# An MLA encoder layer in split fp32: latent keys and gate by seven products of quarters, rotary queries behind the gates

## The chip, the cores and the metric

The kernel runs on one core of a Trainium2 chip. The metric is the device time of one execution, in microseconds (us); a measurement is the median of its runs. Engines are named as in the profile: PE is TensorE (matrix products), PEld its weight loads, DVE VectorE, ACT ScalarE, POOL GpSimd, SP SyncE, which issues nearly all DMAs.

## The reference

One layer of multi-head latent attention over 1024 tokens of width 1024, with 8 heads, all in fp32:

```python
proj = rms_norm(x, g) @ w_in                  # columns: 384 + 256 + 64 + 1024
c_q, c_kv, k_pe, gate = proj[..., :384], proj[..., 384:640], proj[..., 640:704], proj[..., 704:]
q  = (rms_norm(c_q, q_norm) @ w_uq).reshape(B, L, 8, 192)     # 128 plain + 64 rotary
kv = (rms_norm(c_kv, kv_norm) @ w_ukv).reshape(B, L, 8, 256)  # 128 keys + 128 values
q_pe, k_pe = apply_rope(q_pe), apply_rope(k_pe)               # k_pe is shared by all heads
p = softmax((q_nope @ k_nope.T + q_pe @ k_pe.T) * scale)      # per head, not causal
h = x + ((p @ v) * silu(gate)) @ w_out
out = rms_norm(h, final_norm)
```

## The kernel before

**Number format.** fp32 is carried as two fp32r parts, high and low. `split(raw, hi, lo)` makes the high part by a cast on GpSimd and the low part by `raw - hi` on VectorE; `mm3` forms a product as three matmuls, high x high, high x low, low x high (lines 59, 60, 61). Everything before attention is held transposed: features on the 128 partitions, the 1024 tokens along the free axis, in two halves of 512.

**First stage (4.7 to 38 us).** While x arrives in eight blocks of 128 features, each block is scaled by the layer's gain and split into `xh` and `xl` (128 x 8 x 1024 each), and the three tiles of latent queries are accumulated in six PSUM banks. They are copied out raw into `craw_a`. The row factor of the norm, `rx`, is applied to results later, since it is one number for each token.

**Second stage (38 to 171 us), the one that changes.** Ten tiles of 128 weight columns are streamed from DRAM, two of latent keys and eight of the gate. `stream(m)` loads a tile in two parts (`gwr`), splits it (`gwh`, `gwl`) and does 8 blocks x 2 halves x 3 = 48 matmuls into one PSUM tile of 128 x 1024. ScalarE copies latent keys out to `craw`; `stream_gate` multiplies a gate by `rx_sb` (VectorE, reading PSUM) and applies Silu (ScalarE). Between the tiles stand:

- `rstd_x`: the squares of x by ScalarE, the factor `rx` by small VectorE operations, and `spread`, which turns it into a row on all partitions by writing it to DRAM and reading it back;
- `latent_sums`, `latent_norm`, `latent_scale`: the norms of latent queries and keys, with sums of squares by GpSimd additions and a matmul with ones (`total`), again with hops through DRAM;
- the rotary key (`pe`, 32 matmuls, high weight and low weight side by side), its rotation, `kk_h` and `kk_l`;
- the rotary queries: `rope_half(g, half, w)` is called four times, after gates 1 to 4. Each does 18 matmuls into two PSUM tiles `ab`, four multiplications by cosine and sine (VectorE, reading PSUM), two additions (GpSimd), two copies (ScalarE), two subtractions (VectorE), and writes the results to DRAM by four DMAs, from where attention reads them (`qpe`);
- the splits of latent queries (`cq_h`, `cq_l`) and latent keys (`kv_h`, `kv_l`).

**Attention (171 us on)** starts with the first head's keys, `k<-kv_h,wk_h`, then queries, values, scores, softmax, an exchange by DMA and the product with the values. The output projection, the residual and the final norm end the kernel.

**What sets the order.** The program is written with a tile framework that simulates a timeline and sets each engine's instructions into one fixed sequence from dependencies, priorities (the order of the code) and its own estimates. Tiles come from pools; a tile of a pool that is used up waits until the last reader of the old one is done. Pools here are given room in the order of opening and closing, so a pool that takes the room of another waits for the other's readers too.

Of the kernel before, what the change touches and what calls it, by code (L numbers as in the profile page):

```python
# [29 lines left out]
def kernel(  # L30
# [32 lines left out]
    def split(raw, hi, lo):  # L63
        nc.gpsimd.tensor_scalar(hi, raw, 1.0, 1.0, op0=ALU.mult, op1=ALU.mult)
        nc.vector.tensor_sub(lo, raw, f32(hi))
# [131 lines left out]
    wts = cctx.enter_context(tc.tile_pool(name="wts", bufs=1))
    kvp = cctx.enter_context(tc.tile_pool(name="kvp", bufs=1))
    kv_h = kvp.tile([P, 2, L], F32R, name="kv_h")
    kv_l = kvp.tile([P, 2, L], F32R, name="kv_l")  # L200
    rx_sb = xs.tile([P, L], F32, name="rx_sb")
    small = xs.tile([P, 16, KD], F32, name="small")
    ssx, mx, rx, v_s, s_s, r_s = (small[:, i] for i in range(6))
# [6 lines left out]
        nc.sync.dma_start(row_d[name], compact)  # L210
        nc.sync.dma_start(row, row_of(name).partition_broadcast(P))
# [12 lines left out]

    def latent_sums(ms, name):
        cs, sq = gate[:, 4], gate[:, 5]
        for i, m in enumerate(ms):
            if i == 0:
                nc.scalar.activation(cs, craw[m], AF.Square)
            else:  # L230
                nc.scalar.activation(sq, craw[m], AF.Square)
                nc.gpsimd.tensor_add(cs, cs, sq)
        line = gate[0:1, 6]
        for half in range(2):
            nc.scalar.copy(line[:, halves(half)], total(cs, half, name)[0:1])
        nc.sync.dma_start(row_of(name), line)
# [12 lines left out]
            c = craw[m]  # L249
            nc.vector.scalar_tensor_tensor(c, c, g_sb[:, KD + m:KD + m + 1], row, op0=ALU.mult, op1=ALU.mult)  # L250
# [23 lines left out]
    rstd_x()
    ps = stream(3)
    nc.scalar.copy(craw[3], ps)
    latent_sums((0, 1, 2), "sq")
    ps = stream(4)
    nc.scalar.copy(craw[4], ps)
    latent_norm("sq", QR, "rq", gate[:, 7])  # L280
    latent_sums((3, 4), "sk")

    wr = gp.tile([P, KD, DR], F32, name="wpe_r", tag="gwr", bufs=2)
# [5 lines left out]
    for k in range(KD):  # L291
        w = w_pe[k // 4][:, k % 4].rearrange("p a b -> p (a b)")
        for half in range(2):
            hs = halves(half)
            mm(ps[:, hs], lhsT=w, rhs=xh[:, k, hs], start=k == 0, stop=False)
# [13 lines left out]
    for d in (slice(0, DR), slice(DR, P)):  # L309
        nc.scalar.copy(kk_h[d], kp[0:DR])  # L310
        nc.vector.tensor_sub(kk_l[d], kp[0:DR], f32(kk_h[0:DR]))

    latent_scale((0, 1, 2), gate[:, 7])
    latent_norm("sk", KR, "rk", gate[:, 7])
    cqp = cctx.enter_context(tc.tile_pool(name="cqp", bufs=1))
    cq_h = [cqp.tile([P, L], F32R, name=f"cq_h{m}") for m in range(3)]
    cq_l = [cqp.tile([P, L], F32R, name=f"cq_l{m}") for m in range(3)]
    for m in range(3):
        nc.scalar.copy(cq_h[m], craw[m])
        nc.vector.tensor_sub(cq_l[m], craw[m], f32(cq_h[m]))  # L320
# [23 lines left out]
    def rope_half(g, half, w):  # L344

        hs = halves(half)
        ab = []
        for i in range(2):
            ab.append(acc("ab"))
            for k in range(3):  # L350
                mm3(ab[i], w[i][0][:, k], w[i][1][:, k], cq_h[k][:, hs], cq_l[k][:, hs], k == 0, k == 2)
        cos, sin = rope_sb[:, 0, hs], rope_sb[:, 1, hs]
        for i, (f0, f1, op) in enumerate(((cos, sin, ALU.subtract), (sin, cos, ALU.add))):
            t, hl = rooms[((g * 2 + half) * 2 + i) % len(rooms)]
            t0, t1 = t[:, 0:HT], t[:, HT:L]
            hi, lo = hl[:, 0:HT], hl[:, HT:L]
            nc.vector.tensor_mul(t0, ab[0], f0)
# [3 lines left out]
            nc.vector.tensor_sub(lo.bitcast(F32R), t0, hi)  # L361
            for c, src in ((i, hi), (2 + i, lo)):
                nc.sync.dma_start(qpe_d[g * 4:(g + 1) * 4, c, :, hs], src)

    w_rope = [[load_q(wqp[j], rw) for j in range(2)], None]
    for i in range(1, H):
        stream_gate(i)
        if i == 2:
            w_rope[1] = [load_q(wqp[2 + j]) for j in range(2)]
        if i == 5:  # L370
            latent_scale((3, 4), gate[:, 7])
        if i == 6:
            for m in range(2):
                nc.gpsimd.tensor_scalar(kv_h[:, m], craw[3 + m], 1.0, 1.0, op0=ALU.mult, op1=ALU.mult)
                nc.vector.tensor_sub(kv_l[:, m], craw[3 + m], f32(kv_h[:, m]))
# [430 lines left out]
```

## Time and profile before

| | |
|---|---|
| time, median of three runs | 586.93 us (586.86 to 587.76) |
| profiled execution | 587.4 us, of which the span of instructions is 585.7 |
| TensorE busy | 571.8 us, 98% of the span, 2604 matmuls |
| VectorE busy | 425.4 us, 73% |
| ScalarE busy | 275.5 us, 47% |
| GpSimd busy | 233.8 us, 40% |
| granted TensorE clock, mean over the span | 0.993 |
| HBM | 36.19 MB read, 8.41 MB written |

The page of the profile gives the busy time of each engine and its number of instructions, then the span in 40 equal slices, where a digit is the busy share of a slice in tenths, and last the chain of work that ended last. A row of a single instruction in the trace is: start in us, duration in us, engine, line of the kernel, operation, what it writes, what it reads, shape; in brackets the time for which the engine had stood idle and what ended it. A row of a stretch is: the stretch, its length, then busy time and number of instructions for PE, PEld, DVE, ACT, POOL, the granted clock, the share of the DMA engines, GB/s.

### The profile page before, as it was taken

How to read it: one execution, taken by the hardware profiler on the slowest of the kernel's cores; microseconds unless marked ns; L12 is line 12 of the kernel's file. 1: busy time of each engine (PE TensorE's matmuls, PEld its weight loads, DVE VectorE, ACT ScalarE, POOL GpSimd, SP SyncE). 2: the span in 40 equal slices, each digit the busy share in tenths (PEclk: the TensorE clock that was granted, in tenths of full speed). 3: DMA queues.
4: the chain of work that ended last, by engine and by line, in shares of the span. 5: the costliest groups of instructions: out<-in, count | busy, mean ns of one | idle time of the engine just before them, and what ended most of it. 6: DMA issues, size and time to landing. Idle time of an engine off the chain costs nothing.

```text
span 585.7 us, 7657 instructions
## 1 busy us (share of the span) xinstructions
PE 571.8 (98%) x2604; PEld 472.8 (81%) x2604; DVE 425.4 (73%) x573; ACT 275.5 (47%) x438; POOL 233.8 (40%) x201
## 2 busy tenths in 40 slices
PE   9999999999999999999999999999999979999995
PEld 5888888888888878888888888888888858788885
DVE  4923589475236799988888988898888894984663
ACT  4348463021014455553655455645365662644652
POOL 1623512343102345643553535533434874683000
PEclk9999999999999999999999999999999979999999
DMA  8766221324211448674457464763476458521332
GB/s 263 275 206 245 95 74 38 124 93 141 109 38 46 94 117 193 154 171 109 107 132 179 105 153 109 168 148 94 100 162 147 132 135 213 198 77 54 138 132 107
DMA packets 35962, 78.66 MB, mean 134 GB/s; under 512 B 7314, under 2 KB 11154, under 8 KB 35860
## 3 DMA queue, kind: packets, MB, share of 16 engines
q1 hardware_dynamic: 34628, 76.21, 48.3%
q10 hardware_dynamic: 1296, 1.97, 0.9%
q8 instruction: 20, 0.33, 0.2%
q14 instruction: 18, 0.15, 0.1%
HBM read 36.19 MB, written 8.41 MB: 76 GB/s over the span
## 4 chain that ended last, share of the span: by engine, by line
PE 90%; SPq 3%; DVE 2%; ACT 1%; DMA 1%; issue 1%; POOL 0%; DVEq 0%; ACTq 0%; POOLq 0%
PE g L59 6%; PE g L61 6%; PE g L60 6%; PE o L59 5%; PE o L60 5%; PE o L61 5%; PE pv L60 5%; PE pv L59 5%; PE pv L61 5%; PE s L59 4%; PE s L60 4%; PE s L459 4%; PE s L61 4%; PE s L458 4%; SPq L481 3%; PE q L59 2%
## 5 line engine op out<-in xcount | busy, mean ns | idle before, releaser
L472 POOL TENSOR_SCALAR probs<-probs,rc 128x1024 f32<-128x1024 f32 x64 | 84.3, 1319 | 113.0 <-DVE rc L471 108.9
L466 ACT ACTIVATE probs<-s,nmx 128x1024 f32<-128x1024 f32 x64 | 71.6, 1118 | 113.3 <-DVE nmx L464 110.4
L473 DVE STREAM_TRANSPOSE probs<-probs 128x1024 f32<-128x1024 f32 x64 | 79.2, 1238 | 15.8 <-POOL probs L472 14.2
L464 DVE TENSOR_REDUCE nmx<-s 128x1 f32<-128x1024 f32 x64 | 76.0, 1207 | 3.8 <-PE s L459 3.7
L488 ACT CAST pt_h<-d 128x1024 fp32r<-128x1024 f32 x64 | 65.3, 1052 | 8.0 <-PE pv L61 4.9
L59 PE MATMUL g<-xh,gwh 128*128 128x512 f32 x160 | 62.2, 389 | 0.0
L60 PE MATMUL g<-xl,gwh 128*128 128x512 f32 x160 | 62.2, 389 | 0.0
L61 PE MATMUL g<-xh,gwl 128*128 128x512 f32 x160 | 62.2, 389 | 0.0
L493 POOL TENSOR_TENSOR pt_l<-d,pt_h 128x512 fp32r<-128x512 f32 x32 | 49.1, 1534 | 26.0 <-ACT pt_h L488 25.3
L60 PE MATMUL pv<-pt_l,v_h 128*128 128x512 f32 x128 | 50.3, 393 | 2.4 <-POOL pt_l L493 2.0
L59 PE MATMUL s<-k_h,q_h 128*128 128x512 f32 x128 | 50.2, 392 | 1.2 <-ACT probs L466 1.2
L490 DVE TENSOR_TENSOR pt_l<-d,pt_h 128x1024 fp32r<-128x1024 f32 x32 | 48.8, 1524 | 3.5 <-ACT pt_h L488 3.3
L59 PE MATMUL pv<-pt_h,v_h 128*128 128x512 f32 x128 | 50.1, 392 | 0.0
L60 PE MATMUL s<-k_l,q_h 128*128 128x512 f32 x128 | 49.9, 390 | 0.0
L61 PE MATMUL pv<-pt_h,v_l 128*128 128x512 f32 x128 | 49.9, 389 | 0.0
L61 PE MATMUL s<-k_h,q_l 128*128 128x512 f32 x128 | 49.9, 389 | 0.0
L458 PE MATMUL s<-kk_h,qpe 128*128 128x512 f32 x128 | 49.8, 389 | 0.0
L459 PE MATMUL s<-kk_l,qpe 128*128 128x512 f32 x128 | 49.8, 389 | 0.0
L59 PE MATMUL o<-woh,o_split 128*128 128x512 f32 (+1 forms) x118 | 45.8, 388 | 2.5 <-ACT o_split L575 2.5
L60 PE MATMUL o<-wol,o_split 128*128 128x512 f32 (+1 forms) x118 | 45.6, 386 | 0.0
L61 PE MATMUL o<-woh,o_split 128*128 128x512 f32 (+1 forms) x118 | 44.5, 383 | 0.0
L576 DVE TENSOR_TENSOR o_split<-gate,o_split 128x512 fp32r<-128x512 f32 (+2 forms) x48 | 32.5, 708 | 9.4 <-ACT o_split L575 9.3
(194 smaller groups left out, 1237.1 us busy)
## 6 DMA issues: line engine op xcount, KB each, us to landing
d<-probs SPq DMA_DIRECT2D x256, 128.0 KB
gwr<-in_wg SPq DMA_DIRECT2D x20, 256.0 KB
craw_b<-in_x SPq DMA_DIRECT2D x8, 512.0 KB
qpe<-qpe_d SPq DMA_DIRECT2D x16, 256.0 KB
wor<-in_wo SPq DMA_DIRECT2D x16, 256.0 KB
xr<-in_x SPq DMA_DIRECT2D x16, 256.0 KB
xr<-in_xT SPq DMA_DIRECT2D x5, 512.0 KB
qpe_d<-craw_a SPq DMA_DIRECT2D x8, 256.0 KB
```

Source lines behind the costliest of these rows:

```text
L59: mm(ps, lhsT=lh, rhs=rh, start=first, stop=False)
L60: mm(ps, lhsT=lh, rhs=rl, start=False, stop=False)
L61: mm(ps, lhsT=ll, rhs=rh, start=False, stop=last)
L458: mm(s[:, ks], lhsT=qpe_s, rhs=kk_h[:, ks], start=False, stop=False)
L459: mm(s[:, ks], lhsT=qpe_s, rhs=kk_l[:, ks], start=False, stop=True)
L464: maxima[u] = nc.vector.tensor_reduce(nmx, s, axis=AX.X, op=ALU.max, negate=True)
L466: exps[u] = nc.scalar.activation(p_t.rearrange("p j k c -> p k j c"), s.rearrange("p (k j c) -> p k j c", k=8, j=4), AF.Exp, bias=nmx, acc ...
L472: nc.gpsimd.tensor_scalar(p_t, p_t, rc, 1.0, op0=ALU.mult, op1=ALU.mult)
L473: nc.vector.transpose(out=p_t, in_=p_t)
L488: nc.scalar.copy(hi, src)
L490: nc.vector.tensor_sub(lo, src, f32(hi))
L493: nc.gpsimd.tensor_sub(lo[:, 2:4], src[:, 2:4], f32(hi[:, 2:4]))
```

## The change

A product of a 2 x 2 block matrix with another takes eight products of blocks in the ordinary way and seven in Strassen's way (here in Winograd's form). Two weight tiles and x are treated as such: the blocks of the weights are (tile a or b) x (first or second half of the features), and those of x are (half of the features) x (half of the tokens): `x11`, `x12`, `x21`, `x22`, each 128 x 4 x 512 for the high and for the low part.

- `combine_x` makes four sums of quarters of x once: t1 = x12 - x11, t2 = x22 - t1, t3 = x22 - x12, t4 = x21 - t2, each out of high and low parts and split again. The scratch `raw` and `low` lies in `gate`; t1, t2, t4 get a pool of their own (`tp`), t3 overwrites x12. In all it has 12 operations on VectorE and 6 on GpSimd, of 128 x 2048 each.
- `pair(a, b, dst_a, dst_b)` replaces two calls of `stream`. It makes four weight sums on VectorE, splits seven weight blocks, does 7 x 12 = 84 matmuls into single PSUM banks (`acc` and `ps_t` in turn) and adds the seven results up in the destination: one ScalarE copy and seven VectorE additions of 128 x 512, each with one operand in PSUM.
- Pairs are latent keys (0, 1), then gates (i, 4 + i) by `pair_gate(i)`, which multiplies by `rx_sb` on GpSimd.
- `rstd_x` is cut in two: `squares_x` as before; `norm_x`, with the hop of `rx` through DRAM, is issued after `combine_x` has made t2.
- The rotary key's products stand ahead of the pairs, and ScalarE copies them out of PSUM; the multiplication by `rx_sb` then reads SBUF.
- Rotary queries, the splits of latent queries and keys, and the rotary weights (now through the pool `gp`) stand behind the last gate pair, in the room that `tp` gives up. The second half of `rope_half` uses `ps_t` for its PSUM tiles.
- Pool `gp` has 4 buffers instead of 3 and 5 for raw weights instead of 2; pool `rw` is gone. The scratch of `latent_sums` moves from `gate` to `home[1]`.

The core of the diff:

```diff
-    def stream(m):
-        ...
-        ps = wide(f"g_{m}")
-        for k in range(KD):
-            for half in range(2):
-                hs = halves(half)
-                mm3(ps[:, hs], wh[k // 4][:, k % 4], wl[k // 4][:, k % 4], xh[:, k, hs], xl[:, k, hs],
-                    k == 0, k == KD - 1)
-        return ps
-
-    def stream_gate(i):
-        ps = stream(6 + i)
-        gt = gate[:, i]
-        nc.vector.tensor_mul(gt, ps, rx_sb)
-        nc.scalar.activation(gt, gt, AF.Silu)
+    def combine(raw, hl):
+        hi, lo = hl
+        nc.gpsimd.tensor_scalar(hi, raw, 1.0, 1.0, op0=ALU.mult, op1=ALU.mult)
+        return nc.vector.tensor_sub(lo, raw, f32(hi))
+
+    def difference(raw, hl):
+        nc.vector.tensor_sub(raw, f32(hl[0]), raw)
+        nc.vector.tensor_add(raw, raw, f32(hl[1]))
+
+    def combine_x():
+        raw, low = (gate[:, i:i + 2].rearrange("p a (b c) -> p (a b) c", c=HT) for i in (2, 6))
+        nc.gpsimd.tensor_sub(low, f32(x12[1]), f32(x11[1]))
+        nc.vector.tensor_sub(raw, f32(x12[0]), f32(x11[0]))
+        nc.vector.tensor_add(raw, raw, low)
+        combine(raw, t1)
+        difference(raw, x22)
+        ready = combine(raw, t2)
+        nc.gpsimd.tensor_sub(low, f32(x22[1]), f32(x12[1]))
+        nc.vector.tensor_add(low, low, f32(x22[0]))
+        nc.vector.tensor_sub(low, low, f32(x12[0]))
+        combine(low, t3)
+        difference(raw, x21)
+        combine(raw, t4)
+        return ready
+
+    def pair(a, b, dst_a, dst_b):
+        ...
+        def product(i, w, x_part):
+            ps = acc("g") if i % 2 == 0 else ps_t.tile([P, HT], F32, name="g", tag="t")
+            for k in range(4):
+                mm3(ps, w[0][:, k], w[1][:, k], x_part[0][:, k], x_part[1][:, k], k == 0, k == 3)
+            return ps
+
+        (c11, c12), (c21, c22) = ((d[:, 0:HT], d[:, HT:L]) for d in (dst_a, dst_b))
+        nc.scalar.copy(c11, product(0, parts(raw[0, 0]), x11))
+        p2 = product(1, parts(raw[0, 1]), x21)
+        nc.vector.tensor_add(s1, raw[1, 0], raw[1, 1])
+        w_5 = parts(s1)
+        nc.vector.tensor_sub(s1, s1, raw[0, 0])
+        nc.vector.tensor_add(c12, product(2, parts(s1), t2), c11)
+        nc.vector.tensor_add(c11, p2, c11)
+        p5 = product(3, w_5, t1)
+        nc.vector.tensor_sub(raw[1, 0], raw[0, 0], raw[1, 0])
+        nc.vector.tensor_add(c21, product(4, parts(raw[1, 0]), t3), c12)
+        nc.vector.tensor_add(c22, p5, c21)
+        nc.vector.tensor_add(c12, p5, c12)
+        nc.vector.tensor_sub(s1, raw[0, 1], s1)
+        nc.vector.tensor_add(c12, product(5, parts(s1), x22), c12)
+        nc.vector.tensor_add(c21, product(6, parts(raw[1, 1]), t4), c21)
+
+    def pair_gate(i):
+        a, b = gate[:, i], gate[:, 4 + i]
+        pair(2 + i, 6 + i, a, b)
+        for g in (a, b):
+            nc.gpsimd.tensor_mul(g, g, rx_sb)
+            nc.scalar.activation(g, g, AF.Silu)
...
+    kp = gate[:, 5]
+    nc.scalar.copy(kp, ps)
+    with tc.issue_after(combine_x().ins):
+        norm_x()
+    pair(0, 1, craw[3], craw[4])
+    latent_sums((0, 1, 2), "sq")
...
-    kp = home[1][:, 3]
-    nc.vector.tensor_mul(kp, ps, rx_sb)
+    nc.vector.tensor_mul(kp, kp, rx_sb)
...
-    w_rope = [[load_q(wqp[j], rw) for j in range(2)], None]
-    for i in range(1, H):
-        stream_gate(i)
-        ...
+    w_rope = [load_rope(wqp[j]) for j in range(4)]
+    for m in range(2):
+        nc.gpsimd.tensor_scalar(kv_h[:, m], craw[3 + m], 1.0, 1.0, op0=ALU.mult, op1=ALU.mult)
+        nc.vector.tensor_sub(kv_l[:, m], craw[3 + m], f32(kv_h[:, m]))
+    for g in range(2):
+        for half in range(2):
+            rope_half(g, half, w_rope[2 * g:2 * g + 2])
```

The order of instructions moves with it; rows of the changed kernel carry its own line numbers (`mm3` is then lines 62 to 64, `split` 67 and 68, `combine` 265 and 266, `difference` 270 and 271, `combine_x` 275 to 283, `pair` 300 to 326, `rope_half` 421 to 442).

VectorE where the first stage ends, before: the copy of the last accumulator, then weight splits of the gate and the rotary key, the sums for the latent norm (`ss_b`) and the small steps towards `rx`.

```order
L192 COPY craw_a<-acc_120 128x512
L65 TENSOR_TENSOR gwl_1_492<-gwr_1_493,gwh_1_491 128x512
L65 TENSOR_TENSOR wpe_582<-wpe_r,wpe_582 128x4x64
L133 TENSOR_TENSOR ss_b<-ss_t,ss_b 64x512
L220 TENSOR_SCALAR small<-small 128x8
```

The same place now: `gate` is the scratch of `combine_x`, `t_l` the low half of t1, t2 and t4, `gws_465` a weight sum.

```order
L194 COPY craw_a<-acc_117 128x512
L276 TENSOR_TENSOR gate<-xh 128x2048
L277 TENSOR_TENSOR gate<-gate 128x2048
L68 TENSOR_TENSOR gwl<-gws_465,gwh 128x512
L316 TENSOR_TENSOR gws_465<-gws_465,gwr_0_457 128x512
L266 TENSOR_TENSOR t_l<-gate,t_h 128x2048
L270 TENSOR_TENSOR gate<-xh,gate 128x2048
L282 TENSOR_TENSOR gate<-gate,xh 128x2048
L271 TENSOR_TENSOR gate<-gate,xl 128x2048
L68 TENSOR_TENSOR gwl<-gws_465,gwh 128x512
L68 TENSOR_TENSOR gwl<-gwr_0_459,gwh 128x512
L283 TENSOR_TENSOR gate<-gate,xh 128x2048
```

Twelve operations of 128 x 2048 have come in, mixed with the first pair's weight sums and splits; the small steps towards `rx` stand behind the second subtraction for `t_l`.

GpSimd at the same place, before and then now (`wh` is the last weight block of the first stage, `t_h` the high half of t1, then of t2):

```order
L64 TENSOR_SCALAR wh_331<-wr_327 128x384
L64 TENSOR_SCALAR wk_h<-wk_r 128x256
L232 TENSOR_TENSOR gate<-gate 128x1024
L64 TENSOR_SCALAR gwh_1_491<-gwr_1_493 128x512
L232 TENSOR_TENSOR gate<-gate 128x1024
```

```order
L67 TENSOR_SCALAR wh_328<-wr_324 128x384
L275 TENSOR_TENSOR gate<-xl 128x2048
L67 TENSOR_SCALAR gwh<-gws_465 128x512
L265 TENSOR_SCALAR t_h<-gate 128x2048
L281 TENSOR_TENSOR gate<-xl 128x2048
L67 TENSOR_SCALAR gwh<-gws_465 128x512
L67 TENSOR_SCALAR gwh<-gwr_0_459 128x512
L231 TENSOR_TENSOR craw_b<-craw_b 128x1024 x2
L265 TENSOR_SCALAR t_h<-gate 128x2048
```

The additions for the latent sums (L232, now L231) stand between the high halves of t1 and t2.

TensorE at the hand-over to attention, with what a row waits for in brackets (by the engine that releases it), before and then now:

```order
L59 MATMUL g_1283<-xh,gwh_1_1277 128x512
L60 MATMUL g_1283<-xl,gwh_1_1277 128x512
L61 MATMUL g_1283<-xh,gwl_1_1278 128x512
L59 MATMUL k<-kv_h,wk_h 128x512 [waits Activation_49]
L60 MATMUL k<-kv_l,wk_h 128x512
```

```order
L62 MATMUL ab<-cq_h_1265,wrope_h 128x512
L63 MATMUL ab<-cq_l_1268,wrope_h 128x512
L64 MATMUL ab<-cq_h_1265,wrope_l 128x512
L62 MATMUL k<-kv_h,wk_h 128x512 [waits DVE_49,PE_49]
L63 MATMUL k<-kv_l,wk_h 128x512
```

VectorE's last rows ahead of that key product now:

```order
L437 TENSOR_TENSOR craw_a<-ab,craw_b 128x512 [waits Pool_49]
L440 TENSOR_TENSOR craw_b<-craw_a,craw_b 128x512 [waits DMAHW4_49,Activation_49]
L68 TENSOR_TENSOR wq_l<-wq_r,wq_h 128x384 [waits DMAHW5_49,Pool_49]
L436 TENSOR_TENSOR craw_a<-ab,craw_b 128x512 [waits DVE_49]
L440 TENSOR_TENSOR craw_a<-craw_a 128x512 [waits DMAHW0_49,Activation_49]
L440 TENSOR_TENSOR craw_b<-craw_a,craw_b 128x512 [waits DMAHW2_49,Activation_49]
L492 TENSOR_TENSOR k_l<-k,k_h 128x512 [waits Activation_49]
```

Before, the last products ahead of the keys were those of gate 7 and the key waited for ScalarE; now they are the last rotary queries, and the key waits for VectorE's last reading of their PSUM tiles (L436).

More of the change, by code (lines that the diff above doesn't have):

```diff
@@ L232, in latent_sums @@
                 nc.gpsimd.tensor_add(cs, cs, sq)
-        line = gate[0:1, 6]
+        line = home[1][0:1, 3]
         for half in range(2):
@@ L268, in stream_gate, with quarter @@
-    def stream_gate(i):
-        ps = stream(6 + i)
-        gt = gate[:, i]
-        nc.vector.tensor_mul(gt, ps, rx_sb)
-        nc.scalar.activation(gt, gt, AF.Silu)
[L274 to L285, printed above, removed]
+    def quarter(i, j):
+        return tuple(t[:, 4 * i:4 * i + 4, halves(j)] for t in (xh, xl))
@@ new lines @@
+    x11, x12, x21, x22 = (quarter(i, j) for i in range(2) for j in range(2))
+    tctx = ExitStack()
+    tp = tctx.enter_context(tc.tile_pool(name="tp", bufs=1))
+    t2, t1, t4 = (
+        tuple(tp.tile([P, 4, HT], F32R, name=f"{n}_{c}") for c in "hl") for n in ("t2", "t1", "t4")
+    )
+    t3 = x12
+    def combine(raw, hl):
[5 more added lines that the diff above has]
+        nc.vector.tensor_add(raw, raw, f32(hl[1]))
@@ new lines, in pair, with parts @@
+    def pair(a, b, dst_a, dst_b):
+        raw = {}
+        for i, w in enumerate((a, b)):
+            for j in range(2):
+                raw[i, j] = gp.tile([P, 4, P], F32, name=f"gwr_{w}_{j}", tag="gwr", bufs=5)
+        for i, j in ((0, 0), (0, 1), (1, 0), (1, 1)):
+            nc.sync.dma_start(raw[i, j], wg[(a, b)[i], :, 4 * j:4 * j + 4])
+        s1 = gp.tile([P, 4, P], F32, name=f"gws_{a}", tag="gwr", bufs=5)
+        def parts(src):
+            wh = gp.tile([P, 4, P], F32R, name="gwh", tag="gwh")
+            wl = gp.tile([P, 4, P], F32R, name="gwl", tag="gwl")
+            split(src, wh, wl)
+            return wh, wl
+        def product(i, w, x_part):
[19 more added lines that the diff above has]
+        nc.vector.tensor_add(c21, product(6, parts(raw[1, 1]), t4), c21)
@@ L286 @@
+    def pair_gate(i):
[4 more added lines that the diff above has]
+            nc.scalar.activation(g, g, AF.Silu)
+    squares_x()
+    wr = gp.tile([P, KD, DR], F32, name="wpe_r", tag="gwr", bufs=5)
     nc.sync.dma_start(wr, wpe)
@@ L320 @@
         nc.vector.tensor_sub(cq_l[m], craw[m], f32(cq_h[m]))
-    stream_gate(0)
+    kvp = cctx.enter_context(tc.tile_pool(name="kvp", bufs=1))
+    wts = cctx.enter_context(tc.tile_pool(name="wts", bufs=1))
+    kv_h = kvp.tile([P, 2, L], F32R, name="kv_h")
+    kv_l = kvp.tile([P, 2, L], F32R, name="kv_l")
     def load_split(shape, src, tag, bufs, pool=None, raw=None):
@@ L329, in load_split, with load_q, load_rope @@
         return wh, wl
-    def load_q(src, pool=None):
-        return load_split([P, 3, P], src, "wq", 2, pool, pool)
+    def load_q(src):
+        return load_split([P, 3, P], src, "wq", 2)
+    def load_rope(src):
+        wr = gp.tile([P, 3, P], F32, name="wrope_r", tag="gwr", bufs=5)
+        wh = gp.tile([P, 3, P], F32R, name="wrope_h", tag="gwh")
+        wl = gp.tile([P, 3, P], F32R, name="wrope_l", tag="gwl")
+        nc.sync.dma_start(wr, src)
+        split(wr, wh, wl)
+        return wh, wl
     def load_k(h):
@@ L348, in rope_half @@
         for i in range(2):
-            ab.append(acc("ab"))
+            ab.append(acc("ab") if half == 0 else ps_t.tile([P, HT], F32, name="ab", tag="t"))
             for k in range(3):
```

44 lines of the change are left out of this document (15 added, 29 removed).

## The prediction

> **What bounds the kernel now.** I read the page first (busy shares, slices, chain), then the stretch between the first stage and attention, then single tiles for prices.
>
> ```profile
> PE 571.8 (98%) x2604; PEld 472.8 (81%) x2604; DVE 425.4 (73%) x573; ACT 275.5 (47%) x438; POOL 233.8 (40%) x201
> ...
> PEclk9999999999999999999999999999999979999999
> ...
> PE 90%; SPq 3%; DVE 2%; ACT 1%; DMA 1%; issue 1%; POOL 0%; DVEq 0%; ACTq 0%; POOLq 0%
> ```
>
> TensorE is busy 98% of the span, at full clock in all slices but one, and carries 90% of the chain. So fewer matmuls shorten the kernel, if TensorE goes on without waits.
>
> ```profile
> 38.12 0.69 DVE L192 COPY craw_a<-acc 128x512 f32<-128x512 f32 x1
> 171.36 0.39 PE L59 MATMUL k<-kv_h,wk_h 128*128 128x512 f32 x1
> 38.00:171.36 133.36, 133.36 (x589) 110.24 (x588) 69.86 (x93) 49.00 (x66) 41.56 (x37) 1.00 0.33 110
> L59 PE MATMUL g<-xh,gwh x160: 389/389/389, 37.9 to 170.7; 128*128 128x512 f32 x160
> L59 PE MATMUL ab<-cq_h,wq_h x24: 389/389/497, 89.6 to 138.0; 128*128 128x512 f32 x24
> L295 PE MATMUL pe<-xh,wpe 128*128 128x512 f32 x16 | 6.2, 389 | 0.0
> ```
>
> The stage that changes runs from 38.0 (the last first-stage accumulator is copied at 38.12) to 171.36, the first key product of attention. The third row is a stretch of time: TensorE never idles in it, 589 matmuls in 133.36, so one costs 0.2264 us (the 389 ns of the tile rows are overlapped durations). VectorE is busy 70 us there, GpSimd 42, so both have room today. The products are 3 x 160 for the ten weight tiles, 3 x 24 for the rotary queries, 32 for the rotary key.
>
> **What the change removes.** Per pair 7 products x 4 x 3 = 84 matmuls instead of 96, so 60 fewer in five pairs: 60 x 0.2264 = **13.6 us**. This is the whole gain. The eight gate scalings of VectorE (1.2 each) move to GpSimd.
>
> **What it adds: VectorE and GpSimd work, and these two exclude each other.** That is the crux, and rows show it:
>
> ```profile
> 112.86 1.06 POOL L374 TENSOR_SCALAR kv_h<-craw_b 128x1024 fp32r<-128x1024 f32 x1
> 112.94 2.05 DVE L375 TENSOR_TENSOR kv_l<-craw_a,kv_h 128x1024 fp32r<-128x1024 f32 x1 [0.95 <-POOL kv_h L374]
> 113.88 1.59 POOL L64 TENSOR_SCALAR gwh<-gwr 128x512 fp32r<-128x512 f32 x1
> 114.92 1.63 DVE L375 TENSOR_TENSOR kv_l<-craw_b,kv_h 128x1024 fp32r<-128x1024 f32 x1
> ...
> 49.20 1.29 POOL L131 TENSOR_TENSOR ss_t<-ss_t,gate 64x512 f32<-64x512 f32 x1
> 49.27 1.51 DVE L65 TENSOR_TENSOR wpe<-wpe_r,wpe 128x256 fp32r<-128x256 f32 x1 [4.49 <-POOL wpe L64]
> 56.11 0.42 DVE L65 TENSOR_TENSOR wpe<-wpe_r,wpe 128x256 fp32r<-128x256 f32 x1
> ```
>
> GpSimd's cast ends at 113.92; VectorE's subtraction, begun at 112.94, ends 1.07 later, at 114.99; GpSimd's next cast, begun at 113.88, ends 0.48 after that; the next subtraction ends (116.55) 1.08 after that. They take turns. The 256-column subtraction takes 0.42 alone and 1.51 behind GpSimd's addition. So a VectorE operation with two inputs in SBUF holds 1.07 per 1024 columns (0.53 for 512, 2.13 for 2048), and a GpSimd cast 0.48 for 512.
>
> ```profile
> L320 DVE TENSOR_TENSOR cq_l<-craw_a,cq_h x3: 1207/1207/1208, 85.4 to 87.7; 128x1024 fp32r<-128x1024 f32 x3
> L65 DVE TENSOR_TENSOR gwl<-gwr,gwh x20: 639/691/1126, 16.7 to 161.9; 128x512 fp32r<-128x512 f32 x20
> L64 POOL TENSOR_SCALAR gwh<-gwr x20: 617/624/1592, 15.1 to 161.3; 128x512 fp32r<-128x512 f32 x20
> L232 POOL TENSOR_TENSOR gate<-gate x3: 2393/2409/2410, 41.1 to 62.4; 128x1024 f32<-128x1024 f32 x3
> L357 DVE TENSOR_TENSOR craw_a<-ab,craw_b x8: 673/677/684, 94.1 to 141.6; 128x512 f32<-128x512 f32 x8
> ```
>
> Columns are least/median/greatest ns. Alone, VectorE needs 1.21 for 1024 and 0.69 for 512, 0.15 more than it holds. Taking the same off GpSimd: its two-input operation holds 2.25 per 1024 (1.1 for 512, 4.5 for 2048), its cast 0.9 per 1024 (1.8 for 2048). VectorE reading one operand from PSUM (L357) shows 0.68 without spread: it is not held up.
>
> The Trainium skill, page "SBUF — State Buffer", section "Who interferes with whom", says the same of a VectorE instruction with two SBUF inputs against a GpSimd one that reads SBUF, and that the loser blocks for the whole instruction. By whole durations the first sum below would be 66 instead of 60 and the time 647; the rows above show the smaller hold, and I use it.
>
> **First sum: x blocks.** The first operations (`combine_x`) wait for the last first-stage matmul (buffer reuse, and VectorE's copies stand ahead), so start at 38.0. Up to the low half of t4, in program order, on VectorE: 12 operations of 2048 (25.6), 12 of 512 (weight splits and sums, 6.4), 3 PSUM additions (2.0). On GpSimd: 2 subtractions of 2048 (9.0), 4 casts of 2048 (7.2), 7 weight casts (3.4), the two latent sums L231 (4.5) and two half sums L133 (2.2), which stand between. Sum 60.3, ending at 98.3, and nothing of it is parallel but the PSUM additions. Meanwhile TensorE has 12 + 32 + 12 matmuls that need no combination (12.7 us, to 50.7), then waits for t1 (its low half: about 57), t2 (about 79.5), t3 (about 86), t4. After the third PSUM addition (about 95) 35 matmuls remain, 7.9 us, and its clock has dropped:
>
> ```profile
> PE o L59 <- ACT o_split L575: 2.5, 1, 2.5
> 474.00:477.00 3.00, 0.54 (x3) 0.15 (x1) 3.00 (x7) 2.84 (x6) 0.22 (x1) 0.68 0.87 268
> 477.00:479.00 2.00, 2.00 (x5) 1.36 (x6) 2.00 (x4) 2.00 (x3) 1.88 (x2) 0.50 0.06 25
> 481.00:482.00 1.00, 1.00 (x4) 0.81 (x3) 1.00 (x2) 0.20 (x1) 1.00 (x1) 0.54 0.00 0
> 482.00:483.00 1.00, 1.00 (x6) 0.81 (x5) 1.00 (x2) 0.24 (x1) 1.00 (x2) 1.00 0.00 0
> ```
>
> The one 2.5 us wait of today (around 475) was followed by a granted clock of 0.50 until about 481.8: near 4.9 us at half rate, a loss of 2.4. (The Trainium skill, page "TensorE: Matmul & The Clock Gate", Part 1, puts the needed idle time and the slow time at about 3.4 us each, a loss of 1.7; this row shows a shorter wait and a longer loss. With 1.7 at each of three places the time would be 2 us less.) So these 128 matmuls end at 95 + 7.9 + 2.4 = 105.3; without waits 38.0 + 128 x 0.2264 = 67.0. **Wait 1: 38.3.**
>
> **Second sum: latent keys end, first gates, rotary key.** From 98.3 to the second key sum, for which TensorE stops: VectorE 16 of 512 (8.5), 7 of 1024 for the rotary key (7.5), 11 PSUM additions (7.5), ten tiny ones (1.7); GpSimd 8 casts (3.8), L231 (2.25), 2 L133 (2.2), 2 gate scalings (4.5). VectorE also meets, in order, a multiplication by the row factor rx, now made only after `combine_x` and spread through DRAM:
>
> ```profile
> 73.05 0.47 DVE L244 TENSOR_TENSOR small<-small 128x8 f32<-128x8 f32 x1
> 73.54 0.33 SPq L210 DMA_DIRECT2D rq_d<-small  x1
> 74.94 0.33 SPq L211 DMA_DIRECT2D gate<-rq_d  x1
> 78.86 1.35 DVE L250 SCALAR_TENSOR_TENSOR craw_a<-craw_a,g_sb,gate 128x1024 f32<-128x1024 f32 x1 [1.67 <-DMA gate<-rq_d]
> ```
>
> Such a hop takes 5.3 (73.5 to 78.9); work ready meanwhile covers 1.9, leaving 3.4. Sum 41.4, less 2.5 of PSUM additions beside GpSimd: 38.9, to 137.2. TensorE's 87 matmuls alone would end at 105.3 + 19.7 = 125.0. **Wait 2: 12.2.**
>
> **The other three pairs.** Per pair VectorE holds 11 x 0.53, GpSimd 7 x 0.48 + 2 x 2.25: 13.7 against 84 x 0.2264 = 19.0 of TensorE. TensorE sets the pace again: 240 x 0.2264 = 54.3, plus 2.4 of slow clock and about 2 for short waits: 195.9. **Wait 3: 4.4.**
>
> **Rotary queries, moved behind the gates.** Today their vector work lies under gate products. Now TensorE's 72 matmuls (16.3, to 212.2) have only themselves as cover, and the first key product waits for VectorE's last read of their PSUM tiles. From the last product with t4 (193.2) VectorE and GpSimd first make the splits of latent queries and keys: 5 of 1024 (5.4), small splits (1.1), two PSUM additions (1.4), GpSimd casts (2.7) and the last two gate scalings (4.5), 0.7 side by side: 14.4. Then 16 multiplications from PSUM (10.9), 6 subtractions (3.2), three weight splits (1.3) and some 2.5 behind GpSimd's additions: 17.9. So keys begin at 225.5. SP's queue now has four rotary weights, key, query and value weights and eight writes here in a row; a write that isn't back in time already cost VectorE this much:
>
> ```profile
> DVE craw_b L361 <- DMA qpe_d<-craw_b: 6.7, 2, 4.9
> ```
>
> I take none of it. **Wait 4: 13.3** (225.5 - 212.2); bounds: 0 if TensorE covers all, 20 with the 6.7 added.
>
> **Sum.** Waits 38.3 + 12.2 + 4.4 + 13.3 = 68.2, less 13.6: +54.6 at most; by clock, keys at 225.5 instead of 171.4: +54.1. Attention keeps its instructions. The profiled execution took 587.4 (span 585.7); the median of the runs is 586.93, 0.1% less. 587.4 + 54 = **641 us**.
>
> **Rivals.**
> 1. *VectorE's and GpSimd's turns overlap by half.* The L65 median (0.69, its price alone) speaks for it: most meetings pass unharmed. Against it: in the first sum both queues are full. Half of GpSimd's holds go: wait 1 about 25, wait 2 about 6, 3, and 7: 41 - 13.6 = +27, **615**.
> 2. *No exclusion.* By durations alone t2 would be ready at 65: wait 1 about 18, wait 4 about 5: +9.5, **597**. The kv rows speak against it.
> 3. *Faster.* One mechanism: `combine_x` costs only VectorE's own time, GpSimd's share lying under it. Place: TensorE at t2. VectorE's 34 us of the first sum then end at 73, TensorE's part at about 75: wait 8, -13.6 + 8 = **582**. It decides the sign where all waits together stay under 13.6. TensorE has 15.4 us of cover up to t2, and the eight big operations before it take 17.0 alone, so it needs all of GpSimd's part to vanish.
> 4. *Worse.* The pairs fall behind too: a wait in each of three at half clock (3 x 2.4), the 6.7 of late writes, and attention's start at half clock: **660** or more.
>
> **Chances.** Main 0.62 (625 to 660), half 0.15, no exclusion 0.09, faster 0.05, worse 0.07, unmoved 0.02. The range 606 to 662 takes in the main case and most of rival 1. Within 0.2% (1.2 us) is what a measurement here can't tell from no change: 0.02; faster 0.05; slower 0.93.
>
> **What would show it.** TensorE's row: 2544 instructions, no wait before about 50, then waits released by t1, t2, t3, t4 of some 6, 17, 2 and 5, granted clock 0.5 behind them; the slices from 38 to 105 with TensorE at half or less and VectorE and GpSimd both full, big subtractions stretched from 2.25 to between 4 and 7. First key product near 225. It is wrong if those subtractions stay near 2.25 beside busy GpSimd, or if TensorE's wait ahead of t2 is under 5.

## The result, and the profile after

The changed kernel takes 674.88 us (median of 4 runs, 671.74 to 677.32) against 587.35 (586.86 to 588.06): ratio 1.149, 95% interval 1.143 to 1.155. It is slower, as forecast, but by 87.5 us and not by 54, and outside the range. The profiled execution took 671.74, its span is 669.9. That execution was the fastest of the four; the median lies 0.5%, 3 us, above it, and the table of points below is made from it.

The page of the changed kernel: busy time, the slices of TensorE and its clock, the chain by engine.

```profile
PE 579.8 (87%) x2544; PEld 470.8 (70%) x2544; DVE 526.1 (79%) x647; ACT 278.3 (42%) x442; POOL 298.2 (45%) x230
...
PE   9992369589989058999999999999999997999996
...
PEclk9996579879999579999999999999999998999999
...
PE 48%; DVE 25%; DMA 9%; issue 6%; POOL 4%; ACT 4%; SPq 3%; DVEq 0%; ACTq 0%; POOLq 0%
```

60 matmuls fewer, as the diff says, but TensorE's slices now have holes (slices 4 to 6, 8, and 14 to 15), its clock falls at the long ones, and half of the chain has left it: 25% is VectorE's (2% before) and 9% are transfers (1% before). The chain has these four long pieces around the hand-over to attention (start, length):

```profile
213.98 10.87 DMA qpe_d<-craw_b
226.27 10.30 DMA wq_r<-in_wqn
237.63 11.08 DMA qpe_d<-craw_b
250.46 9.33 DMA wq_r<-in_wqn
```

Two are writes of rotary queries and two are query weights issued behind such writes: 41.6 us in all, where the prediction had put nothing. TensorE's longest waits (us in total, times, longest), and the stretch by stages:

```profile
PE k L62 <- DVE craw_a L436: 22.4, 1, 22.4
PE g L63 <- DVE t_l L266: 13.6, 2, 7.5
PE g L62 <- POOL t_h L265: 13.0, 2, 9.9
PE sum_sk L137 <- DVE ss_b L135: 10.7, 2, 8.6
...
38.00:99.00 61.00, 31.27 (x101) 23.26 (x100) 60.76 (x33) 16.27 (x26) 43.10 (x17) 0.71 0.22 69
99.00:137.00 38.00, 27.43 (x116) 21.95 (x114) 35.84 (x44) 15.64 (x20) 19.39 (x15) 0.86 0.23 76
137.00:194.00 57.00, 56.88 (x241) 46.65 (x242) 47.17 (x64) 11.81 (x14) 25.89 (x25) 0.96 0.21 69
194.00:239.60 45.60, 19.35 (x74) 14.28 (x73) 30.49 (x33) 6.90 (x10) 21.08 (x16) 0.75 0.23 79
```

Up to 99 us VectorE is never idle and TensorE half the time; from 137 to 194 TensorE is full again; in the last stretch neither is.

| point (us) | predicted | measured |
|---|---|---|
| low half of t4 made | 98.3 | 99.0 |
| second sum for the latent keys made | 137.2 | 137.1 |
| gate products done | 195.9 | 194.2 |
| rotary products done | 212.2 | 217.2 |
| first key product | 225.5 | 239.6 |
| from there to the end of the span (414.3 before) | 414.3 | 430.3 |

The measured ends come from these rows (the last is the first softmax maximum, 22.6 behind the first key; before it was 11.2 behind):

```profile
96.76 2.28 DVE L266 TENSOR_TENSOR t_l<-gate,t_h 128x2048 fp32r<-128x2048 f32 x1
136.38 0.68 DVE L135 TENSOR_TENSOR ss_b<-ss_t,ss_b 64x512 fp32r<-64x512 f32 x1
194.22 0.84 PE L62 MATMUL ab<-cq_h,wrope_h 128*128 128x512 f32 x3
216.84 0.39 PE L64 MATMUL ab<-cq_h,wrope_l 128*128 128x512 f32 x1
239.61 0.77 PE L62 MATMUL k<-kv_h,wk_h 128*128 128x512 f32 x1 [22.38 <-DVE craw_a L436]
262.17 2.35 DVE L536 TENSOR_REDUCE nmx<-s 128x1 f32<-128x1024 f32 x2
182.54 1.23 DVE L464 TENSOR_REDUCE nmx<-s 128x1 f32<-128x1024 f32 x1 [0.55 <-PE s L459]
```

So the forecast held to 2 us at each of these points until the gates were done, and the whole miss of this execution, 30 us (14.1 to the first key, 16.0 behind it), arose where the rotary queries had been moved to and in attention behind them.

**The exclusion of VectorE and GpSimd** can be read off the first operations:

```profile
37.97 4.62 POOL L275 TENSOR_TENSOR gate<-xl 128x2048 f32<-128x2048 f32 x1 [11.69 <-PE acc L64]
38.48 6.27 DVE L276 TENSOR_TENSOR gate<-xh 128x2048 f32<-128x2048 f32 x1
42.57 2.66 POOL L67 TENSOR_SCALAR gwh<-gws 128x512 fp32r<-128x512 f32 x1
```

GpSimd's subtraction ends at 42.59, VectorE's 2.16 later (44.75), GpSimd's cast of 0.62 another 0.48 later (45.23). Each waits for the other, and what it then needs is the hold that the prediction took from the rows of before (2.13 and 0.48).

**The hand-over.** VectorE's subtraction for the low part of a rotary query (L440) overwrites the buffer of the call of `rope_half` before and waits until that has been written to DRAM; the multiplications behind it in VectorE's queue (L436), whose reading of PSUM the first key waits for, wait along:

```profile
219.82 0.69 DVE L440 TENSOR_TENSOR craw_a<-craw_a 128x512 fp32r<-128x512 f32 x1 [3.99 <-DMA qpe_d<-craw_a]
224.94 0.69 DVE L440 TENSOR_TENSOR craw_b<-craw_a,craw_b 128x512 fp32r<-128x512 f32 x1 [3.23 <-DMA qpe_d<-craw_b]
236.16 0.69 DVE L440 TENSOR_TENSOR craw_b<-craw_a,craw_b 128x512 fp32r<-128x512 f32 x1 [4.07 <-DMA qpe_d<-craw_b]
243.64 0.69 DVE L440 TENSOR_TENSOR craw_a<-craw_a 128x512 fp32r<-128x512 f32 x1 [4.17 <-DMA qpe_d<-craw_a]
...
217.00:225.00 8.00, 0.23 (x2) 0.00 (x0) 1.95 (x4) 1.24 (x2) 1.88 (x2) 0.71 0.26 102
```

While these writes run, the 16 DMA engines are busy 0.26 of the time and move 102 GB/s, with little else under way: as much as four of them would do. At that rate 256 KB (128 x 512 fp32) take 2.6 us and the 16 writes 41.

### The profile page after: what moved, and what is told of

Read it like the earlier page. It is cut to its first block, busy times and chain, and to the rows that moved or that the text cites. A ratio compares the mean times of both kernels' runs of the same rounds, so it can differ in the third digit from the quotient of the medians.

```text
span 669.9 us, 7701 instructions
## 1 busy us (share of the span) xinstructions
PE 579.8 (87%) x2544; PEld 470.8 (70%) x2544; DVE 526.1 (79%) x647; ACT 278.3 (42%) x442; POOL 298.2 (45%) x230
## 4 chain that ended last, share of the span: by engine, by line
PE 48%; DVE 25%; DMA 9%; issue 6%; POOL 4%; ACT 4%; SPq 3%; DVEq 0%; ACTq 0%; POOLq 0%
PE o L62 4%; PE o L63 4%; PE o L64 4%; DMA qpe_d<-craw_b 3%; DMA wq_r<-in_wqn 3%; DVE probs L545 3%; POOL probs L544 3%; SPq L553 3%; PE g L63 3%; PE g L64 3%; PE g L62 3%; PE s L62 2%; DVE nmx L536 2%; ACT probs L538 2%; PE s L64 2%
## 5 line engine op out<-in xcount | busy, mean ns | idle before, releaser
L545 DVE STREAM_TRANSPOSE probs<-probs 128x1024 f32<-128x1024 f32 x64 | 79.2, 1237 | 15.8 <-POOL probs L544 14.8
L565 POOL TENSOR_TENSOR pt_l<-d,pt_h 128x512 fp32r<-128x512 f32 x32 | 45.7, 1428 | 22.5 <-ACT pt_h L560 22.0
L562 DVE TENSOR_TENSOR pt_l<-d,pt_h 128x1024 fp32r<-128x1024 f32 x32 | 51.1, 1597 | 4.6 <-ACT pt_h L560 4.5
L62 PE MATMUL o<-woh,o_split 128*128 128x512 f32 (+1 forms) x118 | 45.2, 383 | 2.5 <-ACT o_split L647 2.5
L63 PE MATMUL g<-t_l,gwh 128*128 128x512 f32 x60 | 25.1, 421 | 13.6 <-DVE t_l L266 13.6
L62 PE MATMUL g<-t_h,gwh 128*128 128x512 f32 x60 | 25.3, 424 | 13.0 <-POOL t_h L265 13.0
L63 PE MATMUL g<-xl,gwh 128*128 128x512 f32 x80 | 33.6, 420 | 2.7 <-DVE xl L266 2.7
```

The costliest lines, as they stand in the source:

```text
L62: mm(ps, lhsT=lh, rhs=rh, start=first, stop=False)
L63: mm(ps, lhsT=lh, rhs=rl, start=False, stop=False)
L545: nc.vector.transpose(out=p_t, in_=p_t)
L562: nc.vector.tensor_sub(lo, src, f32(hi))
L565: nc.gpsimd.tensor_sub(lo[:, 2:4], src[:, 2:4], f32(hi[:, 2:4]))
```

## The experiments

Each kernel was compared with the kernel before on the same chip; the medians of before lie between 587.3 and 588.2.

| run | what | us | ratio, interval |
|---|---|---|---|
| a_rows | changed, layout of the rotary tensor | 653.98 | 1.112 (1.110 to 1.114) |
| a_rows4 | same, reads split | 649.60 | 1.105 (1.103 to 1.108) |
| a_no_pool | changed, sums of quarters without GpSimd | 666.62 | 1.133 (1.131 to 1.136) |
| a_gate_dve | changed, gate scalings on VectorE | 670.44 | 1.143 (1.138 to 1.147) |
| a_keys8 | changed, latent keys by eight products | 667.66 | 1.136 (1.133 to 1.139) |
| a_nocomb | changed, no sums of quarters | 645.16 | 1.097 (1.095 to 1.099) |
| a_all | changed, the first five edits together | 628.75 | 1.070 (1.066 to 1.073) |
| b_late | before, rotary queries behind the gates | 622.24 | 1.058 (1.056 to 1.060) |
| b_late_rows | same, layout | 600.94 | 1.023 (1.021 to 1.024) |
| b_late_rows4 | same, layout and split reads | 599.39 | 1.021 (1.019 to 1.024) |
| b_rows | before, layout | 592.97 | 1.008 (1.007 to 1.010) |
| b_rows4 | before, layout and split reads | 587.46 | 1.001 (0.999 to 1.002) |

### The writes of the rotary queries

`a_rows`, the changed kernel with

```diff
-    qpe_d = dram.tile([H, 4, 32, L], F32, name="qpe_d")
+    qpe_d = dram.tile([4, H, 32, L], F32, name="qpe_d")
-                nc.sync.dma_start(qpe_d[g * 4:(g + 1) * 4, c, :, hs], src)
+                nc.sync.dma_start(qpe_d[c, g * 4:(g + 1) * 4, :, hs].rearrange("h p t -> (h p) t"), src)
-        nc.sync.dma_start(f32(qpe), qpe_d[h, :, :, halves(half)].rearrange("c p t -> (c p) t"))
+        nc.sync.dma_start(f32(qpe), qpe_d[:, h, :, halves(half)])
```

> The changed kernel with one thing altered: the DRAM tensor of the rotary queries is laid out (part, head, feature, token), so that each write of a rotary half is one run of 128 rows instead of 4 runs of 32. In the changed kernel the stretch of these writes (211 to 251 us) shows the DMA engines at 0.22 to 0.25 and about 103 GB/s, as if 4 of the 16 engines worked: 256 KB in 2.5 us, 16 writes in 40 us. Theory 1 (the writes' rate sets the hand-over): the writes shrink to about a quarter, VectorE's and ScalarE's waits for them (22 us and 31 us) go, the first key product comes at 222 to 228 instead of 239.6 and most of the 15.8 us lost behind it return: 671.7 - 14 - 12 = about 646 (640 to 652). Theory 2 (a write takes its 4 to 5 us whatever its layout, and two buffers are too few): no change, 668 to 677. Theory 3 (VectorE's own sums set the hand-over, the writes only lie beside them): 665 to 672.

20.9 us less. The first key came at 228.6 (11.0 earlier, 3.1 behind the forecast) and the rest took 6.8 less; the DMA engines' share in the stretch of the writes rose from 0.26 to 0.63, the rate from 102 to 212 GB/s, and the wait of the first key halved:

```profile
217.00:224.00 7.00, 0.20 (x1) 0.00 (x0) 6.97 (x9) 1.25 (x3) 3.51 (x3) 0.74 0.63 212
PE k L62 <- DVE craw_a L436: 11.4, 1, 11.4
...
228.64 0.77 PE L62 MATMUL k<-kv_h,wk_h 128*128 128x512 f32 x1 [11.45 <-DVE craw_a L436]
```

Theories 2 and 3 are out. Theory 1 is right on the writes but gave 640 to 652, 2 us too little: now VectorE is the full one (6.97 of 7 us), and the reads, which have four runs in this layout, may cost something of their own. `b_rows`, the kernel before with the same three lines, prices those:

> The kernel before with the DRAM layout alone. VectorE and ScalarE wait 11 us for these writes there, but TensorE does not wait in that stage. Theory 1 (the gates cover the writes): no change, 586.5 to 588.5. Theory 2 (the slower spread of the reads, now 4 runs of 32 rows, shows in attention): 590 or more.

It became 5 us slower, theory 2. VectorE waits for a query weight whose load is queued behind the first two reads (first row; the second is the same wait before, 0.64):

```profile
182.02 0.56 DVE L65 TENSOR_TENSOR wq_l<-wq_r,wq_h 128x384 fp32r<-128x384 f32 x1 [5.38 <-POOL wq_h L64]
177.82 0.56 DVE L65 TENSOR_TENSOR wq_l<-wq_r,wq_h 128x384 fp32r<-128x384 f32 x1 [0.64 <-POOL wq_h L64]
```

So each read was cut into four DMAs of 32 rows:

```diff
-        nc.sync.dma_start(f32(qpe), qpe_d[:, h, :, halves(half)])
+        for c in range(4):
+            nc.sync.dma_start(f32(qpe[c * 32:(c + 1) * 32]), qpe_d[c, h, :, halves(half)])
```

> The kernel before with this layout and the split reads. Theory 1: the 5 us that the layout cost come back and nothing is gained, since the gates cover the writes: 586.5 to 589. Theory 2 (the loss was not the reads' four runs): 591 to 594.

> The changed kernel with the DRAM layout of a_rows (writes as one run of 128 rows) and each read of rotary queries as four DMAs of 32 rows instead of one with 4 runs. With the layout alone the time was 654.0; it made the kernel before 5 us slower (593.0), where VectorE waited 5.4 us for a query weight issued behind the first two reads. Theory 1 (reads with 4 runs keep 4 engines busy and delay what is queued behind them at attention's start): 654 - 5 = 649 (646 to 651). Theory 2 (the rest of the loss behind the keys is the clock and the order): 653 to 656.

587.46 and 649.60: theory 1 in both. The kernel before gains nothing from faster writes (1.001, interval 0.999 to 1.002), since its gates cover them; in the changed kernel writes and reads together were worth 25 us.

### The placement alone

`b_late`, the kernel before with the four rotary halves behind the last gate:

```diff
-        if i < 5:
-            g, half = (i - 1) // 2, (i - 1) % 2
-            rope_half(g, half, w_rope[g])
+    w_rope = [load_q(wqp[j], rw) if j < 2 else load_rope(wqp[j]) for j in range(4)]
+    for g in range(2):
+        for half in range(2):
+            rope_half(g, half, w_rope[2 * g:2 * g + 2])
```

> The kernel before, with only the second part of the change: the four rotary halves stand behind the last gate tile, the second half of each in the other PSUM pool, as in the changed kernel; products stay in eight. Theory 1 (the writes of the rotary queries, 16 x 2.5 us, need the gates as cover): TensorE's rotary products begin at 171.4 - 16.3 = 155, first writes at about 160, keys 28 us later as in the changed kernel, 188 (+17), and some 12 to 16 more are lost behind the first keys: 587 + 30 = 617 (608 to 622). Theory 2 (this part is harmless unless VectorE is full of sums of quarters): 587 to 594.

34 us more (622.24), theory 1 at its upper end: without a single sum of quarters, the move costs 40% of what the whole change does. TensorE waits 16.5 ahead of the first key, and again twice behind it, for the low part of a key that stands behind the same writes in VectorE's queue:

```profile
PE k L59 <- DVE craw_a L365: 16.5, 1, 16.5
...
PE k L59 <- DVE k_l L426: 3.5, 1, 3.5
PE q L59 <- DVE k_l L426: 3.1, 1, 3.1
```

`b_late_rows` and `b_late_rows4` add the layout, then the split reads.

> The kernel before with the rotary halves behind the gates (622.2 by itself) and, in addition, the DRAM layout in which a write is one run of 128 rows. In the changed kernel this layout brought the first key forward by 10.8 us and shortened the rest by 6.9. Theory 1 (the same writes set the hand-over here, with no sums of quarters about): 622 - 18 = 604 (598 to 609), so the placement alone still costs some 15. Theory 2 (here the wait is VectorE's or TensorE's own): 615 or more.

> The kernel before with the rotary halves behind the gates, this layout and the split reads (with the layout alone 600.9). Theory 1: 594 to 598, so that of the 34 us that the placement costs about 26 are transfers with 4 runs and 8 are VectorE's sums, of which nothing lies under gate products any more. Theory 2: 600 to 602.

600.94 and 599.39. (By the traces the layout brought the changed kernel 11.0 and 6.8, not 10.8 and 6.9; theory 1 is the same.) The writes were 21 of the 34 us. What the split reads bring, 1.5, is not clear of noise (the two intervals overlap), and 599.39 lies between the two theories; 12 us remain. In the trace of `b_late_rows4` the first key comes at 177.9, 6.6 later than before, behind a wait of 6.0 for VectorE's last reading of PSUM; the rest follows the first key, and its parts were not told apart.

### The sums of quarters

`a_no_pool` takes the sums off GpSimd:

```diff
-        nc.gpsimd.tensor_scalar(hi, raw, 1.0, 1.0, op0=ALU.mult, op1=ALU.mult)
+        nc.scalar.copy(hi, raw)
-        nc.gpsimd.tensor_sub(low, f32(x12[1]), f32(x11[1]))
+        nc.vector.tensor_sub(low, f32(x12[1]), f32(x11[1]))
-        nc.gpsimd.tensor_sub(low, f32(x22[1]), f32(x12[1]))
+        nc.vector.tensor_sub(low, f32(x22[1]), f32(x12[1]))
```

> The changed kernel with the sums of quarters of x taken off GpSimd: the four casts of 128 x 2048 on ScalarE, the two subtractions of 128 x 2048 on VectorE. VectorE then has 14 instead of 12 operations of 128 x 2048. Theory 1 (VectorE's two-input operations and GpSimd take turns, so GpSimd's 16.2 us stood in VectorE's path): VectorE holds 14 x 2.13 + 12 x 0.53 + 2, GpSimd's remaining casts and additions some 8: the low half of t4 comes at 84 to 89 instead of 99.0, VectorE's operations of 128 x 2048 fall from as much as 6.6 us to 2.3 to 4, and the time falls by 8 to 13: 659 to 664. Theory 2 (they are long for another reason, the quarters' stride or the 2048 columns): two more of them make it 5 to 9 slower, 677 to 681.

8.3 us less, theory 1 (2.6 us short of its range), although VectorE has two big operations more. The low half of t4 is ready at 89.1 instead of 99.0. The subtraction that took 6.27 takes 2.70; one that meets a GpSimd addition left there is long again:

```profile
41.15 2.70 DVE L276 TENSOR_TENSOR gate<-xh 128x2048 f32<-128x2048 f32 x1
64.61 4.43 DVE L271 TENSOR_TENSOR gate<-gate,xl 128x2048 f32<-128x2048 f32 x1
86.80 2.28 DVE L266 TENSOR_TENSOR t_l<-gate,t_h 128x2048 fp32r<-128x2048 f32 x1
64.12 2.77 POOL L231 TENSOR_TENSOR craw_b<-craw_b 128x1024 f32<-128x1024 f32 x1
```

`a_gate_dve` puts the eight scalings on VectorE (`nc.gpsimd.tensor_mul(g, g, rx_sb)` becomes `nc.vector.tensor_mul(g, g, rx_sb)`).

> The changed kernel with the eight gate scalings by the row factor back on VectorE (two inputs in SBUF) instead of GpSimd. Theory 1 (VectorE and GpSimd take turns): a scaling costs the pair of engines 1.07 us instead of 2.25, so a move onto the busier engine makes it faster: 4 of the 8 lie where both are the bound, 2 to 7 us less, 665 to 671. Theory 2 (the engines work side by side): VectorE gets 9.7 us more where it is the bound and it is 2 to 6 slower, 677 or more.

670.44, inside theory 1's range, but its interval (1.138 to 1.147) and that of the changed kernel (1.143 to 1.155) overlap. What is shown is that 8 more operations on the busier engine did not make it slower by 2 us or more; the waits of TensorE for the second latent sum fell from 10.7 to 2.1, and other waits took most of that.

`a_nocomb` leaves the sums out (t1 to t4 are quarters of x, so latent keys and gates are other numbers):

```diff
-    t3 = x12
+    t1, t2, t3, t4 = x12, x22, x12, x21
-    with tc.issue_after(combine_x().ins):
-        norm_x()
+    norm_x()
```

> The changed kernel without the sums of quarters of x: t1 to t4 are replaced by quarters of x itself, so the latent keys and gates are not those of the reference; everything else is as in the changed kernel. It prices the sums. Theory 1 (wait 1 of the prediction, 38 to 39 us, is theirs alone): 671.7 - 39 = 633 (626 to 640), TensorE without a wait from 38 to the end of the first pair; the later waits stay: about 11 us at the second latent sum, 22 us ahead of the first key. Theory 2 (the first pair's weight sums and casts and the latent sums are late as well): the gain is under 25, 647 or more.

29.7 us less, between the theories: the 39 us of wait 1 were not the sums' alone. Part of what they hid is now seen. TensorE waits for the weights' splits and for the sum of the latent queries, for which it did not wait in the changed kernel, and of its wait for the latent keys' sum (10.7 there) 7.2 are left:

```profile
PE g L64 <- DVE gwl L68: 8.2, 3, 4.7
PE sum_sk L137 <- DVE ss_b L135: 7.2, 1, 7.2
PE g L62 <- POOL gwh L67: 4.5, 2, 3.9
PE sum_sq L137 <- DVE ss_b L135: 2.3, 1, 2.3
```

So even with the sums for nothing the changed kernel is 23 us slower than `b_late`, which has 60 matmuls more: what is left of the change, such as splitting seven weight blocks, summing four and adding up seven results in each pair, in a stage with the norms and the rotary key, costs more than the 13.6 us. Its parts were not told apart.

`a_keys8` makes latent keys by eight products, ahead of the first pair, as cover for the sums.

```diff
+    for m in range(2):
+        nc.scalar.copy(craw[3 + m], stream(m))
-    pair(0, 1, craw[3], craw[4])
```

> The changed kernel with the two latent key tiles by eight products as before, and only the gates by seven; the key products (96 matmuls) stand ahead of the first pair. 12 matmuls more (2.7 us). Theory 1 (what is lost to the sums of quarters is cover: TensorE has nothing to do meanwhile): TensorE works 96 + 32 matmuls to 67 and 24 more to 72, t2 comes at about 77, so the first pair ends at about 105 as now, but with 84 more matmuls done: 19 us less, 650 to 658. Theory 2 (the whole stage is bound by VectorE and GpSimd together, cover or not): only the first pair's sums and splits go, some 10 us, of which 2.7 come back: 665 to 671.

7.2 us less, theory 2. TensorE did 159 matmuls between 38 and 99 instead of 101, but the low half of t4 came at 96.5, only 2.5 earlier, and the waits moved: 13.0 for the sums of the latent queries, 4.7 for the rotary key's weights, 5.9 and 2.8 for additions of the first gate pair. More cover alone did not help this stage; it is bound by what VectorE and GpSimd have to do.

`a_all` joins layout, split reads, `a_no_pool`, `a_gate_dve` and `a_keys8`.

> The changed kernel with all edits that made it faster: layout and split reads, sums of quarters without GpSimd, gate scalings on VectorE, latent keys by eight products. Singly they brought 21 to 26, 8, 4 and 7 us. Theory 1 (VectorE and GpSimd share one bound, so what is taken off either adds up: 12 us of turns by the sums, 9 by the scalings, 10 by the keys, and 25 by the transfers): 612 to 626. Theory 2 (they uncover one another's waits and do not add): 630 to 640. Neither reaches 587.

628.75: 46.1 us less, where the edits singly brought 25.3 + 8.3 + 4.4 + 7.2 = 45.2 (the 4.4 not clear of noise). They add up, but not to the sum of turns saved (theory 1, 612 to 626), and theory 2's 630 to 640 is missed by a little; neither range held. It is 41 us slower than the kernel before. No kernel here beats that one.

## Why the prediction was wrong

Right were the sign and the mechanism up to the gates. TensorE did wait in the order given, for t1, t2, t3, t4, 6.1, 17.4, 2.7 and 3.1 us against 6, 17, 2 and 5:

```profile
56.88 0.80 PE L63 MATMUL g<-t_l,gwh 128*128 128x512 f32 x1 [6.13 <-DVE t_l L266]
70.95 0.79 PE L62 MATMUL g<-t_h,gwh 128*128 128x512 f32 x1 [9.90 <-POOL t_h L265]
79.26 0.79 PE L63 MATMUL g<-t_l,gwh 128*128 128x512 f32 x1 [7.51 <-DVE t_l L266]
87.03 0.70 PE L63 MATMUL g<-xl,gwh 128*128 128x512 f32 x1 [2.68 <-DVE xl L266]
94.48 0.79 PE L62 MATMUL g<-t_h,gwh 128*128 128x512 f32 x1 [3.07 <-POOL t_h L265]
```

- **First and second sum, pairs (waits 1 to 3).** 0.7, 0.1 and 1.7 us off at their ends. The hold times, taken from one meeting of four instructions in the trace of before, carried 60 us of queue. That the first end is so close is in part luck: VectorE also ran six operations there that the sum leaves out (the first sum for the latent queries and small steps, 2.3 us), and GpSimd, busy 43.1 of the 61.0 us, was not full, though the prediction had expected it full. The Trainium skill, page "SBUF — State Buffer", section "Who interferes with whom", names this lock, held for the whole instruction. The rows agree that the loser blocks, but the lock held 2.16 us where the whole instruction takes 2.28. Wait 1 is not the price of the sums alone: taken out, they gave back 29.7 and not 38.3.
- **Wait 4, the step that failed.** The prediction saw SP's queue with "eight writes here in a row" (they are sixteen), quoted 6.7 us of waits for two of them, wrote "I take none of it", and kept 20 as the upper bound of this term. Measured: the hand-over from the end of the gates to the first key took 45.4 us instead of 29.6, 15.8 more, and the runs show the writes in its place: with the layout alone, 11.0 of this and 6.8 behind the first key went. The rotary products' end, 5.0 behind the forecast, is not due to the writes: it came at 217.2 in `a_rows` too.
- **"Attention keeps its instructions".** It keeps them, but takes 430.3 instead of 414.3. 11.4 of the 16.0 were lost before the first softmax maximum, where low parts of keys and queries stood behind the same writes in VectorE's queue and query weights behind them in SP's. The last 4.6 fall later in attention and were not traced further. The measured time lies in the fourth rival's "660 or more", but only a part of its mechanism came: late writes, at 17.8 by the layout alone instead of its 6.7, and half clock at attention's start (0.50 from 239.6 to 244.0), while the pairs did not fall behind.
- **What the trace of before could have told.** The two waits of 4.9 and 1.8 that made up the 6.7 stood in a stage where one rotary half came every 9 to 24 us. Sixteen writes in one stretch have to be priced by their rate, not by a wait that cover had shortened. The rate was there to be read, in a stretch of the kernel before with two pairs of these writes and nothing else, under TensorE's full slices:

```profile
145.50:150.50 5.00, 5.00 (x23) 4.13 (x22) 2.47 (x4) 0.62 (x1) 1.83 (x3) 1.00 0.26 102
```

The same 0.26 and 102 as after: 2.6 us for each write, 41 for sixteen.

By the runs, the 87.5 us are 34 for the placement (21 of them the writes) and, by difference, some 53 for the seven products, of which the sums of quarters were 30. The prediction had 13.3 for the first and 41.3 for the second. The two parts do not meet at the same place of the trace: the prediction's wait 4 also holds the latent splits and the last gate scalings, which stand elsewhere in `b_late`.

With the transfers mended (`a_rows4`, 649.60) the time lies inside the forecast range, 9 us above the point. In its trace the first key comes at 227.9, 2.4 behind the forecast, and 6.2 more are lost behind it; what causes these stays open.

## What to carry to other kernels

When a step is moved out from under cover, price its transfers by bytes over the rate that this very transfer shows, all of them in a row, and follow the queues behind their buffers; a short wait seen under cover is no price. A product saved on TensorE is worth its 0.23 us only where the engines that make its operands have time: here 13.6 us of matmuls were bought with 30 us for the sums of quarters alone, in a stage where VectorE had been busy half the time and GpSimd a third. An experiment that leaves the suspected part out prices it better than its own wait does, since other waits move up.

## What the runs showed of the hardware

- A DMA between 128 partitions of SBUF and a DRAM block of 4 x 32 rows ran at 102 GB/s with the engines busy 0.26; the same 256 KB against 128 rows in one run went in a stretch with 0.63 and 212 GB/s. The Trainium skill, page "DMA: Bandwidth & Descriptors", section "Why a DMA increments its semaphore by 16 and not by 1", says that the number of engines is the largest up to 16 that divides the slowest dimension of both sides, so 4 here; the share agrees. By this rule, which the prediction left out, and the rate above, sixteen writes would have been priced at some 41 us, an estimate.
- After a wait TensorE ran at a granted clock of 0.50 to 0.52, and a matmul took 0.63 instead of 0.39 us: after 6.1 us without a matmul from 56.9 to 60.0, after 9.9 and 7.5 with one matmul between from 79.2 to 83.7, after 2.7 from 87.0 to 90.5, after 2.3 from 200.2 to 203.3, after 22.4 from 239.6 to 244.0. These are 3.1 to 4.5 us, less than the 4.9 that the prediction took from the one wait of before. After 3.1 us, with a second wait of 0.4 close behind, it lasted longer, from 94.4 to 100.6. Waits of 2 to 3 us were enough.
